# Feed-forward entries of a two-layer decoder: ScalarE empties the PSUM banks, and the first entry's normalisation takes its statistics from summed residuals and squares

## The chip, the cores and the metric

The kernel runs on one core of a Trainium2 chip. The metric is the device time of one execution in microseconds; the time of a kernel is the median of its runs. The core's engines are TensorE (PE, with its weight load PEld), VectorE (DVE), ScalarE (ACT), GpSimd (POOL) and SyncE (SP), which issues most of the transfers.

## The reference

Input and output are 1024 tokens of 1024 features in fp32. Two layers run one after the other; layer 0 mixes tokens by a gated linear recurrence, layer 1 by sliding-window attention. Each mixer ends in a projection `w_out`, and each layer ends in a gated feed-forward network of width 2816 with a causal depthwise convolution. Every sub-layer is joined to the stream in the same way:

```python
def layer_norm(x, g, b):
    mu = xf.mean(-1, keepdims=True)
    var = jnp.square(xf - mu).mean(-1, keepdims=True)
    y = (xf - mu) * lax.rsqrt(var + LN_EPS) * g + b
...
    # each sub-layer: x = layer_norm(ALPHA * x + sublayer(x), g, b)
```

What matters here is the join between a mixer's projection and the feed-forward network behind it: residual sum, normalisation over the 1024 features, and the first products of the network.

## The kernel before, in words

A block `tb` is 128 tokens, so there are 8 blocks; a row tile `Y[:, tb, :]` is 128 x 1024. fp32 matrix products are made as three matmuls (L222 to L224, `mm3`) of a high and a low part: ScalarE casts the high part (`nc.scalar.copy`, L249), VectorE subtracts it to get the low part (L197, `low_part`).

**The entry of a feed-forward network** is `out_proj` with the tasks `Up.ln(tb)` that it starts. `out_proj` makes the mixer's output projection in two halves of 512 columns, `dh` 0 and 1. Each product of a block is 24 matmuls into a 128 x 512 PSUM bank (`psmm`, four banks taken in turn; some of the first half's lie in `psax`). VectorE adds it to the residual (L380) and takes the statistics of that half row (`ln_half`, L263). In the second half the blocks come in the order 4, 5, 6, 7, 0, 1, 2, 3. After a block's second half, `Up.ln` runs `ln_affine`: the two half statistics are aggregated (L269), the variance gets its epsilon (L270), POOL takes the power −0.5 (L271), VectorE subtracts the mean and multiplies with gain (L280), then scales and adds bias (L283), and the rows are stored. Then the block waits until the order clock has gone on by 8 us (blocks 0 to 3) or 13 us (blocks 4 to 7; 10 in layer 1), and TensorE turns it: two halves of four 128 x 128 transposes each (`tr`, L232) into a bank apiece.

What is taken out of these banks: for blocks 0 to 3 the high part (ScalarE), the low part (VectorE, from the bank) and a copy of the turned rows (ScalarE, L433) into `hf`; for blocks 4 to 7 a copy of the first half (L435), and for the second half a high and a low part and the sum with the first half (L438, from the bank). L443 to L445 make further sums of turned blocks. They are the operands of the feed-forward products, in which seven block products stand for eight; the parts of the weights are summed by `weight_sums` (L480 to L483) and split like the rest. `collect` empties the later products' banks (L506 to L520), makes the convolution (L526, L528) and the gate (L531, L533).

**What sets the order.** Only TensorE's order is written by hand. Its work is spaced by a clock `od` that counts estimated work. On the other engines a scheduler orders the instructions by due times and priorities; what stands under `urgent()` is put forward. Each engine then executes in order and stops at the first instruction whose operands or target are not ready.

Names in the lists below: `Y_4374` holds the rows of blocks 4 to 7, `Y_4181` those of blocks 0 to 3, `rx_4698` to `rx_4700` are three tiles into which weights and rows are loaded, `HL` holds split weights (and one row of gains), `T` turned blocks, `st`, `mv` and `rs` are statistics, `gd` the network's hidden rows in HBM.

Of the kernel before, what the change touches and what calls it, by code (L numbers as in the profile page):

```python
# [10 lines left out]
F32 = mybir.dt.float32  # L11
# [5 lines left out]
P = 128  # L17
S = 1024
D = 1024
# [115 lines left out]
def trunk(ctx: ExitStack, tc: tile.TileContext, a: dict, out: bass.AP):  # L135
# [123 lines left out]
    def ln_half(tb, i):  # L259

        if tb not in half_stats:
            half_stats[tb] = sm.tile([P, 2, 6], F32, name="st", bufs=8)
        nc.vector.bn_stats(half_stats[tb][:, i, :], Y[:, tb, i * 512:(i + 1) * 512])  # L263
# [7 lines left out]
        nc.gpsimd.tensor_tensor(rs, rs, nhalf, op=ALU.pow)  # L271
        return mv, rs

    def ln_affine(tb, rows, dst, n=1):

        y = Y[:, tb, :]
        mv, rs = ln_stats(tb)
        parts = [slice(h * D // n, (h + 1) * D // n) for h in range(n)]
        for hs in parts:
            nc.vector.scalar_tensor_tensor(y[:, hs], y[:, hs], mv[:, 0:1], rows[0][:, hs],  # L280
                                           op0=ALU.subtract, op1=ALU.mult)
        for hs in parts:
            nc.vector.scalar_tensor_tensor(y[:, hs], y[:, hs], rs, rows[1][:, hs], op0=ALU.mult, op1=ALU.add)  # L283
            nc.sync.dma_start(dst(hs), y[:, hs])
# [71 lines left out]
    def out_proj(us, begun, rows, resid, ff, ln):  # L356
        tasks, late = [], []
        for tb in range(NB):
            nc.sync.dma_start(Y[:, tb, :], resid(tb))
        for tb, ps in enumerate(begun):  # L360
            out_part(ps, us, tb, [KC - 1])
        for dh in range(2):
            if dh:
                ff.row_loads()
                ff.weights(1)
            for tb in range(NB):
                if dh == 0 and tb < 4:
                    out_late(late, rows, tb, ff.TX)
                elif dh == 0 and tb == 4:
                    ff.weights(0)  # L370
                if dh:
                    tb = (tb + 4) % NB
                if dh == 0 and tb < len(begun):
                    ps = begun[tb]
                else:
                    ps = psmm()
                    out_part(ps, late if dh else us, tb, range(KC))
                y = Y[:, tb, dh * 512:(dh + 1) * 512]
                with urgent() if dh else nullcontext():
                    nc.vector.scalar_tensor_tensor(y, y, ALPHA, ps, op0=ALU.mult, op1=ALU.add)  # L380
                    ln_half(tb, dh)
                if dh == 1:
                    tasks.append(od.spawn(ln(tb)))
                    od.tick()
        return tasks
# [17 lines left out]
    class Up:  # L403
        def __init__(self, l, pool, rx):
            self.l, self.rx = l, rx
            self.wv = a["ffn_w_in"][l].rearrange("(kc p) c -> p kc c", p=P)
            self.TX = pool.tile([P, 2, 2, 4, 512], F32R, name="TX")
            self.T2 = pool.tile([P, 2, 4, 512], F32R, name="T2")
            self.W, self.raw, self.pieces = {}, {}, 0

        def row_loads(self):
# [5 lines left out]

        def ln(self, tb):
            with urgent():
                ln_affine(tb, self.rows, lambda hs: ynd[:, tb, hs], 2 if tb == 3 else 1)  # L420
            yield 8.0 if tb < 4 else 10.0 if self.l else 13.0
            turned = lambda t: (self.rx[2 * t - 4] if t in (2, 3) else Y[:, t, :]).rearrange("p (k t) -> p k t", k=KC)
            hf = turned(tb)
            ts = slice(tb * P, (tb + 1) * P)
            with urgent():
                for q in range(2):
                    ps, ks = psmm(), slice(4 * q, 4 * q + 4)
                    for k in range(4):
                        tr(ps[:, k * P:(k + 1) * P], Y[:, tb, (4 * q + k) * P:(4 * q + k + 1) * P])
                    pv = ps.rearrange("p (k t) -> p k t", k=4)  # L430
                    if tb < 4:
                        split(T[:, 0, ks, ts], T[:, 1, ks, ts], pv)
                        nc.scalar.copy(hf[:, ks], pv)  # L433
                    elif q == 0:
                        nc.scalar.copy(hf[:, ks], pv)  # L435
                    else:
                        split(T[:, 0, ks, ts], T[:, 1, ks, ts], pv)
                        tt(hf[:, ks], hf[:, :4], pv, op=add)  # L438
                        split(T[:, 0, :4, ts], T[:, 1, :4, ts], hf[:, ks])
                        return  # L440
            sf = turned(tb + 4)
            a11, a12, a21, s1 = hf[:, :4], hf[:, 4:], sf[:, :4], sf[:, 4:]
            tt(a21, a11, a21, op=sub)  # L443
            tt(a11, s1, a11, op=sub)
            tt(a12, a12, a11, op=sub)  # L445
            split(self.T2[:, 0, :, ts], self.T2[:, 1, :, ts], a21)
            yield 100.0
            pair = hf.rearrange("p (c k) t -> p c k t", c=2)
            split(self.TX[:, :, 0, :, ts], self.TX[:, :, 1, :, ts], pair)
# [1462 lines left out]
```

## Time and profile before

| | |
|---|---|
| median of 3 runs | 2120.18 us (2120.07 to 2121.75) |
| profiled execution | 2122.24 us, span 2120.4 us |
| mean granted TensorE clock | 0.996 |
| TensorE (PE) busy | 2091.9 us, 99% of the span |
| VectorE (DVE) busy | 1777.2 us, 84% |
| ScalarE (ACT) busy | 968.1 us, 46% |
| GpSimd (POOL) busy | 187.1 us, 9% |

A time in a row of the trace is counted from the span's start. A row of the timeline has start, duration, engine, line, operation, target and operands, shape and type, and in brackets the idle time before it with what ended it. "PEclk" is the granted clock as a share of full speed. Matmuls overlap their neighbours, so their spacing is read from start to start. The entry of layer 0's feed-forward network lies at about 476 to 556 us, that of layer 1's at about 1430 to 1530 us.

### The profile page before, as it was taken

What the parts mean: (1) busy time and instruction counts of PE and PEld (TensorE: products, weight loads), DVE (VectorE), ACT (ScalarE), POOL (GpSimd) and SP (SyncE); (2) the same over time, 40 slices, a digit from 0 to 9 for tenths busy, and PEclk for the clock granted to TensorE, in tenths of its full rate; (3) what the DMA queues carried; (4) which work ended last, traced back from release to release, by engine and by line L of the source; (5) the groups of instructions that cost most, each with busy time, mean ns of one, the idle gap of its engine ahead of it and who ended that gap; (6) DMA issues with size and microseconds to landing.
All of it is one profiled execution on the core that took longest, in us unless ns stands there. A gap on an engine that the chain in (4) does not pass through costs nothing. (4 is left out here: it accounts for less than half of the span.)

```text
span 2120.4 us, 31566 instructions
## 1 busy us (share of the span) xinstructions
PE 2091.9 (99%) x12303; PEld 1742.8 (82%) x12303; DVE 1777.2 (84%) x2420; ACT 968.1 (46%) x1562; POOL 187.1 (9%) x214
## 2 busy tenths in 40 slices
PE   9899999999999999999999999999999999999998
PEld 7688888887878888888888888888888888888886
DVE  6677777769989999888988668979999999978986
ACT  6455565543444444444433356743544444444430
POOL 1000000001010000000001122311010000000002
PEclk9999999999999999999999999999999999999999
DMA  4021111143247765628754511052266776449662
GB/s 153 21 71 50 51 51 51 66 169 110 90 124 174 194 156 150 157 98 294 268 189 159 159 34 38 23 156 93 85 167 167 177 174 161 123 152 326 225 207 98
DMA packets 239823, 286.82 MB, mean 135 GB/s; under 512 B 30216, under 2 KB 160440, under 8 KB 239416
## 3 DMA queue, kind: packets, MB, share of 16 engines
q1 hardware_dynamic: 223360, 238.26, 34.6%
q0 software_dynamic: 15456, 46.16, 10.9%
q8 instruction: 97, 1.59, 0.3%
q14 instruction: 54, 0.44, 0.1%
q10 hardware_dynamic: 856, 0.37, 0.1%
HBM read 241.72 MB, written 89.15 MB: 156 GB/s over the span
## 5 line engine op out<-in xcount | busy, mean ns | idle before, releaser
L222 PE MATMUL psmm<-T,HL 128*128 128x512 f32 x816 | 323.3, 396 | 5.2 <-ACT T L874 4.8
L223 PE MATMUL psmm<-T,HL 128*128 128x512 f32 x816 | 319.2, 391 | 1.3 <-DVE T L197 1.3
L224 PE MATMUL psmm<-T,HL 128*128 128x512 f32 x816 | 319.3, 391 | 0.2 <-DVE HL L197 0.2
L528 DVE SCALAR_TENSOR_TENSOR Y<-Y,cwt,Y 128x1023 f32<-128x1023 f32 (+1 forms) x176 | 225.1, 1281 | 49.7 <-ACT Y L526 48.3
L249 ACT CAST HL<-rx 128x1024 fp32r<-128x1024 f32 (+1 forms) x151 | 151.1, 1006 | 159.6 <-DMA rx<-in_ffn_w_in_dram 28.1
L197 DVE TENSOR_TENSOR HL<-rx,HL 128x1024 fp32r<-128x1024 f32 (+1 forms) x151 | 176.4, 1175 | 17.6 <-ACT HL L249 17.3
L222 PEld LDWEIGHTS psmm<-T,HL 128*128 128x128 f32 x816 | 153.9, 189 | 36.8 <-ACT T L874 5.2
L224 PEld LDWEIGHTS psmm<-T,HL 128*128 128x128 f32 x816 | 153.8, 188 | 33.0 <-DVE HL L197 0.6
L223 PEld LDWEIGHTS psmm<-T,HL 128*128 128x128 f32 x816 | 153.9, 189 | 32.8 <-DVE T L197 2.2
L222 PE MATMUL psax<-T,HL 128*128 128x512 f32 x392 | 153.5, 392 | 0.0
L223 PE MATMUL psax<-T,HL 128*128 128x512 f32 x392 | 152.9, 390 | 0.0
L224 PE MATMUL psax<-T,HL 128*128 128x512 f32 x392 | 152.7, 390 | 0.0
L526 ACT ACTIVATE Y<-Y,cwt 128x1024 f32<-128x1024 f32 x88 | 108.8, 1237 | 92.8 <-DVE Y L515 82.8
L197 DVE TENSOR_TENSOR HL<-raw,HL 128x512 fp32r<-128x512 f32 (+1 forms) x121 | 92.2, 789 | 40.6 <-ACT HL L1296 30.7
L271 POOL TENSOR_TENSOR rs<-rs,nhalf 128x1 f32<-128x1 f32 x32 | 45.0, 1407 | 735.3 <-DVE rs L270 735.3
L249 ACT CAST HT<-rx 128x1024 fp32r<-128x1024 f32 (+1 forms) x37 | 35.5, 960 | 139.2 <-DVE rx L482 61.9
L222 PEld LDWEIGHTS psax<-T,HL 128*128 128x128 f32 x392 | 73.8, 188 | 15.9 <-ACT Y L507 0.4
L222 PE MATMUL psmm<-HL 128*128 128x512 f32 x220 | 86.9, 395 | 0.0
L224 PEld LDWEIGHTS psax<-T,HL 128*128 128x128 f32 x392 | 73.8, 188 | 15.4
L223 PEld LDWEIGHTS psax<-T,HL 128*128 128x128 f32 x392 | 73.8, 188 | 15.2
L223 PE MATMUL psmm<-HL 128*128 128x512 f32 x220 | 85.9, 391 | 0.0
L224 PE MATMUL psmm<-HL 128*128 128x512 f32 x220 | 85.8, 390 | 0.0
(404 smaller groups left out, 5200.5 us busy)
## 6 DMA issues: line engine op xcount, KB each, us to landing
rx<-in_ffn_w_in_dram SPq DMA_DIRECT2D x136, 256.0 KB
rx<-gd SPq DMA_DIRECT2D x118, 256.0 KB
bsd<-in_ffn_w_out_dram POOLq DMA_DIRECT2D x36, 768.0 KB, 8.4
gd<-Y SPq DMA_DIRECT2D x44, 512.0 KB
raw<-in_hgrn_w_in_dram SPq DMA_DIRECT2D x30, 512.0 KB
rx<-in_ffn_w_out_dram SPq DMA_DIRECT2D x54, 256.0 KB
R<-bsd SPq DMA_DIRECT2D x44, 256.0 KB
Y<-in_ffn_w_in_dram SPq DMA_DIRECT2D x40, 256.0 KB
```

The lines of the kernel that those rows point to most:

```text
L197: make = lambda e: e.tensor_tensor(lo, src, hi.bitcast(F32), op=ALU.subtract)
L222: nc.tensor.matmul(ps, st(0), mv(0), start=start, stop=False, skip_group_check=onto)
L223: nc.tensor.matmul(ps, st(0), mv(1), start=False, stop=False, skip_group_check=onto)
L224: nc.tensor.matmul(ps, st(1), mv(0), start=False, stop=stop, skip_group_check=onto)
L249: nc.scalar.copy(hi, src)
L271: nc.gpsimd.tensor_tensor(rs, rs, nhalf, op=ALU.pow)
L526: nc.scalar.activation(c, u, AF.Identity, bias=cwt[:, l, 3, ci:ci + 1], scale=cwt[:, l, 2, ci:ci + 1])
L528: nc.vector.scalar_tensor_tensor(c[:, sh:], u[:, :S - sh], cwt[:, l, 2 - sh, ci:ci + 1], c[:, sh:], op0=ALU.mult, op1=ALU.add)
```

## The change: what it does

Three things are changed in the entries; TensorE's instructions and their order stay as they are.

1. *The second half's products.* ScalarE copies the bank into a new tile `lf` in SBUF (128 x 512, one buffer), and VectorE's residual sum reads `lf` (both layers).
2. *The turned rows.* ScalarE makes the high part and the plain copy of a bank; VectorE makes the low part from the copy in SBUF, and for blocks 4 to 7 the sum with the first half too (both layers).
3. *The statistics, layer 0 only.* The residual sums give out their row sums (`accum_out`); the 16 half-row statistics and 8 aggregations go. VectorE makes the negative mean (L294 of the changed kernel), ScalarE squares the two half rows with the mean as bias and gives out their sums (L296, the squares themselves go to a part of `T` that is not in use then), VectorE adds them (L298), POOL adds epsilon (L299) and takes the power (L300).

```diff
-    def ln_affine(tb, rows, dst, n=1):
+    def resid_half(tb, i, ps, summed):
+        y = Y[:, tb, i * 512:(i + 1) * 512]
+        if not summed:
+            nc.vector.scalar_tensor_tensor(y, y, ALPHA, ps, op0=ALU.mult, op1=ALU.add)
+            ln_half(tb, i)
+            return
+        if tb not in half_stats:
+            half_stats[tb] = sm.tile([P, 2, 6], F32, name="st", bufs=8)
+        nc.vector.scalar_tensor_tensor(y, y, ALPHA, ps, op0=ALU.mult, op1=ALU.add,
+                                       accum_out=half_stats[tb][:, 0, i:i + 1])
+
+    def square_stats(tb):
+        st = half_stats.pop(tb)
+        less = st[:, 0, 2:3]
+        rs = sm.tile([P, 1], F32, name="rs")
+        nc.vector.tensor_scalar(less, st[:, 0, 0:1], st[:, 0, 1:2], -1.0 / D, op0=ALU.add, op1=ALU.mult)
+        for i in range(2):
+            nc.scalar.activation(T[:, 1, :4, tb * P:(tb + 1) * P], fourths(Y[:, tb, i * 512:(i + 1) * 512]), AF.Square, bias=less,
+                                 accum_out=st[:, 1, i:i + 1])
+        nc.vector.tensor_scalar(rs, st[:, 1, 0:1], st[:, 1, 1:2], 1.0 / D, op0=ALU.add, op1=ALU.mult)
+        nc.gpsimd.tensor_scalar(rs, rs, 1.0, LN_EPS, op0=ALU.mult, op1=ALU.add)
+        nc.gpsimd.tensor_tensor(rs, rs, nhalf, op=ALU.pow)
+        return less, rs
+
+    def ln_affine(tb, rows, dst, n=1, summed=False):
         y = Y[:, tb, :]
-        mv, rs = ln_stats(tb)
+        if summed:
+            mean, rs = square_stats(tb)
+            from_it = ALU.add
+        else:
+            mv, rs = ln_stats(tb)
+            mean, from_it = mv[:, 0:1], ALU.subtract
...
-            nc.vector.scalar_tensor_tensor(y[:, hs], y[:, hs], mv[:, 0:1], rows[0][:, hs],
-                                           op0=ALU.subtract, op1=ALU.mult)
+            nc.vector.scalar_tensor_tensor(y[:, hs], y[:, hs], mean, rows[0][:, hs],
+                                           op0=from_it, op1=ALU.mult)
...
-                y = Y[:, tb, dh * 512:(dh + 1) * 512]
                 with urgent() if dh else nullcontext():
-                    nc.vector.scalar_tensor_tensor(y, y, ALPHA, ps, op0=ALU.mult, op1=ALU.add)
-                    ln_half(tb, dh)
+                    if dh:
+                        nc.scalar.copy(ff.left, ps)
+                        ps = ff.left
+                    resid_half(tb, dh, ps, ff.l == 0)
...
+            self.left = pool.tile([P, 512], F32, name="lf")
...
-                    if tb < 4:
-                        split(T[:, 0, ks, ts], T[:, 1, ks, ts], pv)
-                        nc.scalar.copy(hf[:, ks], pv)
-                    elif q == 0:
-                        nc.scalar.copy(hf[:, ks], pv)
-                    else:
-                        split(T[:, 0, ks, ts], T[:, 1, ks, ts], pv)
-                        tt(hf[:, ks], hf[:, :4], pv, op=add)
+                    if tb < 4 or q:
+                        nc.scalar.copy(T[:, 0, ks, ts], pv)
+                    nc.scalar.copy(hf[:, ks], pv)
+                    if tb < 4 or q:
+                        low_part(T[:, 1, ks, ts], hf[:, ks], T[:, 0, ks, ts], None)
+                    if tb >= 4 and q:
+                        tt(hf[:, ks], hf[:, :4], hf[:, ks], op=add)
                         split(T[:, 0, :4, ts], T[:, 1, :4, ts], hf[:, ks])
                         return
```

The scheduler's order on VectorE moves with it. At the place where block 0 is normalised in layer 0 (`Y_4181`), VectorE's rows stood so before:

```order
L380 SCALAR_TENSOR_TENSOR Y_4181<-Y_4181,psmm 128x512
L483 TENSOR_TENSOR rx_4700<-rx_4700,rx_4698 128x512
L197 TENSOR_TENSOR T<-Y_4374,T 128x4x128
L263 BN_STATS st<-Y_4181 128x6
L197 TENSOR_TENSOR T<-psmm,T 128x4x128
L269 BN_AGGR mv<-st 128x2
L438 TENSOR_TENSOR Y_4374<-Y_4374,psmm 128x512
L270 TENSOR_SCALAR rs<-mv 128x1
L280 SCALAR_TENSOR_TENSOR Y_4181<-Y_4181,mv,HL 128x1024
L197 TENSOR_TENSOR T<-Y_4374,T 128x4x128
L283 SCALAR_TENSOR_TENSOR Y_4181<-Y_4181,rs,rx_4699 128x1024
```

and stand so in the changed kernel (its L283 is the residual sum, L314 and L317 are the two steps that were L280 and L283, L473 was L438):

```order
L283 SCALAR_TENSOR_TENSOR Y_4181,st<-Y_4181,lf 128x512
L197 TENSOR_TENSOR T<-Y_4374,T 128x4x128
L294 TENSOR_SCALAR st<-st 128x1
L473 TENSOR_TENSOR Y_4374<-Y_4374 128x512
L197 TENSOR_TENSOR HL<-rx_4698,HL 128x1024
L197 TENSOR_TENSOR T<-Y_4374,T 128x4x128
L298 TENSOR_SCALAR rs<-st 128x1
L314 SCALAR_TENSOR_TENSOR Y_4181<-Y_4181,st,HL 128x1024
L283 SCALAR_TENSOR_TENSOR Y_4181,st<-Y_4181,lf 128x512
L317 SCALAR_TENSOR_TENSOR Y_4181<-Y_4181,rs,rx_4699 128x1024
```

Two rows (L294 and L298) now stand between the residual sum and L314, with ScalarE's squares between them; a low half of weights of 1024 columns (`HL<-rx_4698`) and block 1's residual sum stand ahead of block 0's last step, and another such half (`HL<-rx_4700`) stands some rows further ahead.

ScalarE's rows for the end of the entry, where block 2 is turned and block 3 is normalised, in the changed kernel (L414 is the copy into `lf`, L468 and L469 the high part and the copy of turned rows, L296 the squares):

```order
L414 COPY lf<-psmm 128x512
L468 CAST T<-psmm 128x4x128
L469 COPY rx_4698<-psmm 128x512
L468 CAST T<-psmm 128x4x128
L296 ACTIVATE T,st<-Y_4181,st 128x4x128
L469 COPY rx_4698<-psmm 128x512
L296 ACTIVATE T,st<-Y_4181,st 128x4x128
```

Block 3's squares stand behind casts and copies of block 2. Later, in the fourth of the network's product groups (at about 600 us before), VectorE's rows stood so before:

```order
L482 TENSOR_TENSOR Y_4374<-Y_4374,rx_4700 128x512
L197 TENSOR_TENSOR HL<-rx_4699,HL 128x512
L483 TENSOR_TENSOR rx_4700<-rx_4700,Y_4374 128x512
L528 SCALAR_TENSOR_TENSOR Y_4374<-Y_4181,cwt,Y_4374 128x1023
L518 TENSOR_TENSOR Y_4181<-Y_4181,psmm 128x1024
L528 SCALAR_TENSOR_TENSOR Y_4374<-Y_4181,cwt,Y_4374 128x1022
L520 TENSOR_TENSOR Y_4181<-Y_4181,psax 128x512
L197 TENSOR_TENSOR HL<-rx_4700,HL 128x1024
L197 TENSOR_TENSOR HL<-Y_4374,HL 128x1024
```

and stand so in the changed kernel (L517, L518, L553, L555 and L563 were L482, L483, L518, L520 and L528):

```order
L517 TENSOR_TENSOR Y_4374<-Y_4374,rx_4700 128x512
L563 SCALAR_TENSOR_TENSOR Y_4374<-Y_4181,cwt,Y_4374 128x1023
L548 TENSOR_TENSOR Y_4181<-Y_4181,psax 128x512
L563 SCALAR_TENSOR_TENSOR Y_4374<-Y_4181,cwt,Y_4374 128x1022
L518 TENSOR_TENSOR rx_4700<-rx_4700,Y_4374 128x512
L550 TENSOR_TENSOR Y_4181<-Y_4181,psmm 128x512
L197 TENSOR_TENSOR HL<-Y_4374,HL 128x1024
L197 TENSOR_TENSOR HL<-rx_4700,HL 128x1024
L563 SCALAR_TENSOR_TENSOR Y_4374<-Y_4181,cwt,Y_4374 128x1023
L553 TENSOR_TENSOR Y_4181<-Y_4181,psmm 128x1024
L563 SCALAR_TENSOR_TENSOR Y_4374<-Y_4181,cwt,Y_4374 128x1022
L555 TENSOR_TENSOR Y_4181<-Y_4181,psax 128x512
```

The low half `HL<-Y_4374` stands ahead of the half `HL<-rx_4700` and of four rows (two of the convolution, two sums of products) that it stood behind.

More of the change, by code (lines that the diff above doesn't have):

```diff
@@ L272, in ln_stats, with fourths @@
         return mv, rs
-    def ln_affine(tb, rows, dst, n=1):
-        y = Y[:, tb, :]
-        mv, rs = ln_stats(tb)
+    def resid_half(tb, i, ps, summed):
[8 more added lines that the diff above has]
+                                       accum_out=half_stats[tb][:, 0, i:i + 1])
+    def fourths(v):
+        return v.rearrange("p (k t) -> p k t", k=4)
+    def square_stats(tb):
[11 more added lines that the diff above has]
+    def ln_affine(tb, rows, dst, n=1, summed=False):
+        y = Y[:, tb, :]
+        if summed:
[4 more added lines that the diff above has]
+            mean, from_it = mv[:, 0:1], ALU.subtract
         parts = [slice(h * D // n, (h + 1) * D // n) for h in range(n)]
         for hs in parts:
-            nc.vector.scalar_tensor_tensor(y[:, hs], y[:, hs], mv[:, 0:1], rows[0][:, hs],
-                                           op0=ALU.subtract, op1=ALU.mult)
+            nc.vector.scalar_tensor_tensor(y[:, hs], y[:, hs], mean, rows[0][:, hs],
+                                           op0=from_it, op1=ALU.mult)
         for hs in parts:
@@ L419, in ln @@
             with urgent():
-                ln_affine(tb, self.rows, lambda hs: ynd[:, tb, hs], 2 if tb == 3 else 1)
+                ln_affine(tb, self.rows, lambda hs: ynd[:, tb, hs], 2 if tb == 3 else 1, self.l == 0)
             yield 8.0 if tb < 4 else 10.0 if self.l else 13.0
```

## The prediction

> **What bounds the kernel now.** I read the busy times and the waits of TensorE first, since an engine that is hardly ever idle can only be helped by taking its waits away.
>
> ```profile
> PE 2091.9 (99%) x12303; PEld 1742.8 (82%) x12303; DVE 1777.2 (84%) x2420; ACT 968.1 (46%) x1562; POOL 187.1 (9%) x214
> ```
>
> TensorE is busy 2091.9 of 2120.4 us. The change leaves its instructions and their order as they are, so it can only act through waits (some 28 us in all) and through the granted clock. The waits of TensorE by releaser (total, times, longest) say which of them the change touches:
>
> ```profile
> PE psmm L224 <- DVE HL L197: 2.9, 2, 2.7
> PE psmm L232 <- DVE Y L380: 1.6, 1, 1.6
> ...
> PE psmm L232 <- ACT Y L433: 1.2, 1, 1.2
> ...
> PE psmm L232 <- DVE Y L438: 0.4, 1, 0.4
> ```
>
> L232 are the turning instructions of the first feed-forward entry, which wait for a PSUM bank: L380 is VectorE's residual sum out of a bank, L438 its sum of turned rows, L433 a copy by ScalarE. The first row, 2.7 us in one piece, is a product's wait for the low half of a weight. The entry is the stretch from about 505 to 556 us; its first 36 us by engine (PE, PEld, DVE, ACT, POOL, then clock, DMA share and GB/s):
>
> ```profile
> 505.00:541.00 36.00, 32.52 (x166) 26.71 (x165) 35.70 (x56) 12.46 (x22) 7.32 (x5) 1.00 0.30 117
> ```
>
> VectorE is busy 35.70 of 36.00 there, ScalarE 12.46: a bank that VectorE is to empty stands in VectorE's queue. On TensorE itself:
>
> ```profile
> 516.00 0.60 PE L232 MATMUL psmm<-ident,Y 128*128 128x128 f32 x4
> 518.24 0.66 PE L232 MATMUL psmm<-ident,Y 128*128 128x128 f32 x4 [1.64 <-DVE Y L380]
> ...
> 530.50 1.04 PE L232 MATMUL psmm<-ident,Y 128*128 128x128 f32 x8
> 531.78 1.09 PE L232 MATMUL psmm<-ident,Y 128*128 128x128 f32 x8 [0.24 <-ACT Y L435]
> ```
>
> Eight turns last 1.04 us and four 0.60, so four more cost 0.44. Block 5's second half starts 2.24 us after its first: 1.80 late, 0.16 more than the wait shown. With the same 0.16 the waits of 0.4, 0.24 and 1.2 are 0.6, 0.4 and 1.35 late. **Bank waits of this entry: 4.1 us.**
>
> **What goes.** ScalarE now empties every bank of the entry (bar the early dh=0 products), and on the changed order its copy stands two or three rows behind what TensorE last wrote. So all 4.1 us of bank waits end. That gain is bounded by 0 and 4.1; I take 4.1, because ScalarE has 23 us free in the 36.
>
> The reads that move from PSUM to SBUF gain VectorE nothing:
>
> ```profile
> L263 DVE BATCH_NORM_STATS2 st<-Y 128x6 f32<-128x512 f32 x16 | 10.9, 686 | 0.0
> L197 DVE TENSOR_TENSOR T<-psmm,T 128x512 fp32r<-128x512 f32 x12 | 8.0, 675 | 0.5 <-ACT T L249 0.5
> L197 DVE TENSOR_TENSOR T<-Y,T 128x512 fp32r<-128x512 f32 x5 | 3.4, 687 | 0.0
> ```
>
> 675 ns from PSUM, 687 from SBUF. What VectorE loses is the 16 statistics rows of 686 ns, of which some nine fall behind 497.7 us.
>
> **What comes: the queue ahead of block 0.** Take away the bank waits and TensorE reaches block 0's turns at 531.78 − 0.24 − 1.80 − 0.60, about 529.0 us. They need block 0's normalised rows, and those come from VectorE's queue:
>
> ```profile
> 497.72 1.23 DVE L197 TENSOR_TENSOR HL<-rx,HL 128x1024 fp32r<-128x1024 f32 x1 [2.59 <-ACT HL L249]
> ...
> 501.26 0.20 DVE L269 BATCH_NORM_AGGREGATE mv<-st 128x2 f32<-128x12 f32 x1
> 501.38 0.69 DVE L482 TENSOR_TENSOR rx<-rx,rx 128x512 f32<-128x512 f32 x1
> 501.98 0.15 DVE L270 TENSOR_SCALAR rs<-mv 128x1 f32<-128x1 f32 x1
> 502.05 1.28 DVE L280 SCALAR_TENSOR_TENSOR Y<-Y,mv,HL 128x1024 f32<-128x1024 f32 x1
> 503.24 0.69 DVE L483 TENSOR_TENSOR rx<-rx,rx 128x512 f32<-128x512 f32 x1
> ...
> 529.84 1.28 DVE L283 SCALAR_TENSOR_TENSOR Y<-Y,rs,rx 128x1024 f32<-128x1024 f32 x1
> ```
>
> Start to start, a 512-column operation takes 0.60, a 1024-column one with a scalar 1.19, a tiny one 0.12. Before, block 0 was ready at 531.1; so even an unchanged queue would hold TensorE 2.1 us here. In the changed order the stretch from the row at 497.72 to block 0's last L317 holds 5 low halves of 1024 columns (1.13 each, by the two rows at 609.81 below), 10 operations of 1.19, 24 of 0.60 and 10 tiny ones: 5.65 + 11.9 + 14.4 + 1.2 = 33.2 us. No less than before (33.4, from 497.7 to 531.1), although the statistics are gone: two 1024-column weight halves, HL<-rx_4700 and HL<-rx_4698, now stand ahead of block 0 and stood behind it.
>
> To it come waits inside the queue. Each block's chain leaves VectorE and returns twice: L294 to ScalarE's two squares to L298, then POOL's L299 and L300 to L317. Their prices, by the nearest rows:
>
> ```profile
> L1016 ACT ACTIVATE kp<-fg,one 128x512 f32<-128x512 f32 x14 | 10.1, 722 | 0.5
> L1233 ACT ACTIVATION_READ_ACCUMULATOR sq<-psax 128x1 f32 x64 | 12.5, 196 | 0.0
> ...
> L271 POOL TENSOR_TENSOR rs<-rs,nhalf x32: 919/1452/1537, 502.2 to 2114.6; 128x1 f32<-128x1 f32 x32
> L1234 POOL TENSOR_SCALAR ss<-ss x8: 199/344/909, 114.1 to 468.0; 128x8 f32<-128x8 f32 x8
> ```
>
> Two squares with their read-outs are 2 × (0.72 + 0.20) = 1.84 us, POOL 0.34 + 1.45 = 1.79 where it was 1.45. Between L298 and L317 stand one 1.19 and one 0.60 operation, exactly 1.79, so a wait of 0.2 to 0.3 shows at each of four blocks; one block's L298 finds too little ahead of it, and a weight sum's low half waits for ScalarE's cast. I put 1.9 us for all (bounds 0 and 3). The residual sum with an accumulator has no row; its nearest, ScalarE's, is followed by a read-out row. If VectorE has one too, six lie ahead of block 0 at 0.12: 0.7 us (bounds 0 and 6 × 0.20 = 1.2). I take it. Block 0 is ready at 497.7 + 33.2 + 1.9 + 0.7 = 533.5: **a new wait of 4.5 us** (2.1 to 6.0) takes the place of the 4.1.
>
> **The clock.** One stretch shows a wait long enough to be punished, another one that isn't:
>
> ```profile
> 519.00:520.00 1.00, 1.00 (x6) 0.83 (x5) 1.00 (x3) 1.00 (x2) 0.00 (x0) 1.00 0.67 274
> ...
> 613.00:614.00 1.00, 1.00 (x4) 0.81 (x3) 1.00 (x3) 0.00 (x0) 0.00 (x0) 0.64 1.12 337
> 614.00:615.00 1.00, 1.00 (x4) 0.76 (x3) 1.00 (x1) 0.05 (x1) 0.00 (x0) 0.50 0.89 261
> ```
>
> ```profile
> 608.90 0.39 PE L222 MATMUL psmm<-TX,HL 128*128 128x512 f32 x1
> 609.13 0.39 PE L223 MATMUL psmm<-TX,HL 128*128 128x512 f32 x1
> 612.20 0.50 PE L224 MATMUL psmm<-TX,HL 128*128 128x512 f32 x1 [2.68 <-DVE HL L197]
> ...
> 616.88 0.40 PE L222 MATMUL psax<-T,HL 128*128 128x512 f32 x1
> ...
> 80.75 0.78 PE L222 MATMUL psmm<-T,HL 128*128 128x512 f32 x1 [4.79 <-ACT T L874]
> ...
> 87.63 0.40 PE L224 MATMUL psmm<-HL 128*128 128x512 f32 x1
> ```
>
> After the wait of 1.64 us the granted clock stays 1.00. After 2.68 us it falls to 0.50 at 614, and the 13 steps from 612.20 to 616.88 take 4.68 instead of 13 × 0.23 = 2.95: 1.7 lost. After 4.79 us the 14 steps to 87.63 take 6.88, of which 0.39 is another wait: 3.3 lost. For 4.5 us I take **1.8 us** (0 to 3.3), nearer the lower since turns and products just before keep the array busy. [...]
>
> **The last block.** Block 3's turns have no wait now, but little slack:
>
> ```profile
> 550.59 1.41 DVE L283 SCALAR_TENSOR_TENSOR Y<-Y,rs,rx 128x512 f32<-128x512 f32 x2
> ```
> ```profile
> 552.94 1.04 PE L232 MATMUL psmm<-ident,Y 128*128 128x128 f32 x8
> ```
>
> The rows end at 552.0, the turns start at 552.94: 0.9 us. The chain grows by ScalarE's copy into lf (0.5), the squares (1.84) queued behind a cast and a copy of block 2 (1.0), POOL's 0.34 and two tiny operations (0.2), and loses statistics of 0.6 + 0.2: 3.1 longer, so **2.2 us** late (0 to 3, nothing if ScalarE is free).
>
> **The wait at 609.** The product there stands still for HL<-Y, the second of these two rows:
>
> ```profile
> 601.94 2.62 DVE L482 TENSOR_TENSOR Y<-Y,rx 128x512 f32<-128x512 f32 x1
> ...
> 609.81 1.21 DVE L197 TENSOR_TENSOR HL<-rx,HL 128x1024 fp32r<-128x1024 f32 x1
> 610.94 1.21 DVE L197 TENSOR_TENSOR HL<-Y,HL 128x1024 fp32r<-128x1024 f32 x1
> ```
>
> In the changed order this low half stands ahead of HL<-rx, two convolution rows and two collecting sums that preceded it: 1.13 + 2 × 1.19 + 1.13 + 0.60 = 5.2 us earlier, about 606.9, where 609.4 is needed. The wait with its lateness (612.20 − 609.13 − 0.23 = 2.84) and its slow clock (1.73) go: **−4.6 us**. L482 (now L517) stands earlier too, behind fewer others, and must find its load landed; if not, the wait stays (bounds −4.6 and 0).
>
> **Layer 1's entry** gets the copy and the turned rows only; TensorE has no wait there now, and a chain longer by about 0.5 us stays inside it: 0.
>
> **Sum**: −4.1 + 4.5 + 1.8 + 2.2 − 4.6 = −0.2 us. Against the profiled execution's 2122.24 that is 2122.0. This execution lies 2.06 above the median, so on the median 2120.18 the forecast is **2120.0 us**: no change. About 0.2%, 4.2 us, is what a measurement of this kernel can tell from none.
>
> **Rivals.**
> *Block 0's queue at its floor.* If the accumulator costs nothing, the chain's waits are hidden and ScalarE serves block 3 in time, the terms are −4.1 + 2.1 + 0 + 0 − 4.6 = −6.6: 2113.6. For it: 23 us of idle ScalarE, and a wait of 2.1 lies between the 1.64 that kept the clock and the 2.68 that lost it. Against it: VectorE's in-order waits, four times. Chance 0.33.
> *The accumulating sum is slow (slower).* The residual sum now reads two fp32 arrays in SBUF and accumulates besides. If that takes it to half rate, each takes 0.53 us more (1.13 against 0.60); six before block 0 replace the read-outs' 0.7 by 3.2, the wait there is 7.0, its clock loss 3.3, and block 3 is 1.1 later with two more: −0.2 + 2.5 + 1.5 + 1.1 = +4.9, 2125.1. It decides from some 0.5 us an instruction. Against it: L280 reads two fp32 arrays in SBUF at the full 1.19 for 1024, but without an accumulator. Chance 0.14. [...]
> *The 609 wait stays*, since L517's load lands late: −0.2 + 4.6 = +4.4, 2124.6. Against it: L482 starts at 601.94 without a wait; how long its load had been there, no row shows. Chance 0.08.
> *The banks don't come free.* lf has one buffer, so ScalarE's copy may wait for VectorE's sum of the product before. Then the 4.1 stay as before, and block 0's wait shrinks by the same, since its queue sets its time: −0.2 again, 2120.0. It belongs to the forecast.
>
> **How the numbers follow.** Forecast 0.45, with its own range 2116 to 2124; the floor 0.33, slow accumulator 0.14, 609 wait 0.08. Faster takes the floor's share, all but a little, and the forecast's lower tail: 0.33. Slower takes most of the two last and the forecast's upper tail: 0.22. Same 0.45. The range runs from 2113.0 (a little under the floor rival) to 2125.3 (just above the slow one), which leaves out about a third of the floor's share and half of the slow one's.
>
> **What would show it.** Right: no L232 wait on VectorE's residual sum; a wait of 4 to 5 us at block 0's turns with 0.5 clock behind it; block 3's turns waiting some 2 us for L317; no 2.7 us wait in the fourth product group. Wrong: L283 rows of 1.1 us and more; block 0 ready before 531.5; a wait on lf; or new waits in layer 1's entry.

## The result

The changed kernel is slower: median 2125.72 us (11 runs, 2124.22 to 2128.32) against 2121.20 us for the kernel before on the same chips (11 runs). The ratio is 1.0023, 95% interval 1.0015 to 1.0031. The forecast was 2120.0 us and no change; the measured time lies 0.4 us above the range, and the likeliest case was the wrong one. The kernel before came out 1.0 us above the 2120.18 us on which the forecast stood, so the change itself costs 4.5 us by the medians. The profiled execution took 2125.27 us, its span is 2123.5 us.

The waits of TensorE in the changed kernel, by releaser (total, times, longest):

```profile
PE psmm L232 <- DVE st L294: 6.1, 1, 6.1
...
PE psmm L232 <- DVE Y L317: 1.3, 2, 0.9
...
PE psax L222 <- ACT Y L542: 1.2, 1, 1.2
...
PE psmm L232 <- ACT Y L469: 0.6, 1, 0.6
```

The residual sum, the sum of turned rows and the copies no longer hold TensorE, but for 0.6 us. The 2.7 us wait for a low half is gone. In their place stand one wait of 6.1 us, two for L317, and a new one in layer 1. On TensorE's timeline:

```profile
528.05 1.03 PE L232 MATMUL psmm<-ident,Y 128*128 128x128 f32 x8
535.14 1.94 PE L232 MATMUL psmm<-ident,Y 128*128 128x128 f32 x8 [6.05 <-DVE st L294]
543.47 1.03 PE L232 MATMUL psmm<-ident,Y 128*128 128x128 f32 x8
551.01 1.06 PE L232 MATMUL psmm<-ident,Y 128*128 128x128 f32 x8 [0.36 <-DVE Y L317]
558.48 1.14 PE L232 MATMUL psmm<-ident,Y 128*128 128x128 f32 x8 [0.93 <-DVE Y L317]
```

Block 0's eight turns last 1.94 instead of 1.03 us, and from them to the next block's it is 8.33 us, where 6.33 lie between other blocks (521.72 to 528.05): 2.0 us of slow clock. The first stretch of the entry and the fourth product group in windows (PE, PEld, DVE, ACT, POOL, clock, DMA share, GB/s):

```profile
505.00:541.00 36.00, 29.37 (x141) 24.42 (x141) 31.03 (x49) 22.16 (x47) 11.19 (x11) 0.91 0.25 93
...
600.00:620.00 20.00, 20.00 (x90) 16.57 (x89) 19.12 (x20) 9.00 (x10) 3.60 (x2) 1.00 0.32 106
```

VectorE fell from 35.70 to 31.03 us busy and is no earlier for it: it now stands still between its rows. What it stands still for is seen at block 0's last step:

```profile
531.00 0.21 DVE L298 TENSOR_SCALAR rs<-st 128x1 f32<-128x1 f32 x1
531.13 1.28 DVE L314 SCALAR_TENSOR_TENSOR Y<-Y,st,HL 128x1024 f32<-128x1024 f32 x1
532.32 0.69 DVE L283 SCALAR_TENSOR_TENSOR Y<-Y,lf 128x512 f32<-128x512 f32 x1
532.93 0.08 DVE L283 DVE_READ_ACCUMULATOR Y<-Y,lf 128x1 f32 x1
533.71 1.28 DVE L317 SCALAR_TENSOR_TENSOR Y<-Y,rs,rx 128x1024 f32<-128x1024 f32 x1 [0.70 <-POOL rs L300]
534.91 0.21 DVE L294 TENSOR_SCALAR st<-st 128x1 f32<-128x1 f32 x1
```
```profile
531.30 1.75 POOL L299 TENSOR_SCALAR rs<-rs 128x1 f32<-128x1 f32 x1 [5.87 <-DVE rs L298]
533.14 0.54 POOL L300 TENSOR_TENSOR rs<-rs,nhalf 128x1 f32<-128x1 f32 x1
```

From L298 to L317 it is 2.71 us; the rows between fill 1.8. POOL's two instructions did not run beside these rows. L299 starts 0.17 us behind the start of L314 and ends at 533.05, just behind the second of the rows (533.01), and only then comes the power, L300. In all eight blocks of the entry L299 ends 0.05 us behind the end of a VectorE row whose two tensor operands lie in SBUF: L314 alone, or the row after it too. The power takes 0.54 us when no such row runs; when one does, it takes 0.87 and ends 0.40 us behind the row. Two rows from elsewhere show that it is neither the idle stretch ahead of POOL nor just any row of VectorE. In the changed kernel at 467 us, after 45 us without work, a tiny instruction of POOL takes 0.20 us with VectorE at rest. In e8 (below), where block 1's residual sum reads a bank, the power keeps its 0.54 us beside that sum, and L317 follows 0.1 us behind it:

```profile
467.22 0.20 POOL L1269 TENSOR_SCALAR ss<-ss 128x8 f32<-128x8 f32 x1 [44.95 <-ACT sq L1268]
```
```profile
531.71 0.68 DVE L283 SCALAR_TENSOR_TENSOR Y<-Y,psmm 128x512 f32<-128x512 f32 x1
532.32 0.08 DVE L283 DVE_READ_ACCUMULATOR Y<-Y,psmm 128x1 f32 x1
532.50 1.28 DVE L317 SCALAR_TENSOR_TENSOR Y<-Y,rs,rx 128x1024 f32<-128x1024 f32 x1
```
```profile
531.92 0.54 POOL L300 TENSOR_TENSOR rs<-rs,nhalf 128x1 f32<-128x1 f32 x1
```

In the changed kernel L317 ends at 534.99, and the turns start at 535.14, though the profile puts the wait down to the next row on the queue, L294. Over the whole entry, VectorE's groups say the same:

```profile
L317 DVE SCALAR_TENSOR_TENSOR Y<-Y,rs,rx 128x1024 f32<-128x1024 f32 x7 | 9.0, 1285 | 4.1 <-POOL rs L300 3.4 <-DMA rx<-in_ln_mix_b_dram 0.7
...
L283 DVE SCALAR_TENSOR_TENSOR Y<-Y,lf 128x512 f32<-128x512 f32 x8 | 5.5, 687 | 0.4 <-ACT lf L414 0.4
...
L283 DVE DVE_READ_ACCUMULATOR Y<-Y,lf 128x1 f32 x8 | 0.7, 84 | 0.0
```

L317 waits 3.4 us for POOL, some 0.43 or 0.71 us at a time. The residual sum with an accumulator takes 687 ns from SBUF, as before from PSUM without one (678), and its read-out 84 ns that the next row covers.

In layer 1 ScalarE waits for a load ahead of the copies that empty a bank:

```profile
1569.34 0.62 ACT L249 CAST HT<-rx 128x512 fp32r<-128x512 f32 x1 [6.95 <-DMA rx<-in_ffn_w_in_dram]
...
1571.97 0.56 ACT L541 COPY Y<-psax 128x512 f32<-128x512 f32 x1
1572.43 0.58 ACT L542 COPY Y<-psax 128x512 f32<-128x512 f32 x1
```
```profile
1573.06 0.50 PE L222 MATMUL psax<-T,HL 128*128 128x512 f32 x1 [1.21 <-ACT Y L542]
```

Before, the same cast started at 1566.18, 3.2 us earlier, and TensorE had no wait there. TensorE itself is 1.9 us later here than before, and so is the first issue of the load (first the rows of SyncE's queue before, then of the changed kernel); the other 1.3 us lie between the issue and the cast, and why the load took longer the runs don't show:

```profile
1558.08 3.19 SPq L471 DMA_DIRECT2D rx<-in_ffn_w_in_dram  x4
```
```profile
1559.94 4.01 SPq L506 DMA_DIRECT2D rx<-in_ffn_w_in_dram  x4
```

### The profile page after: what moved, and what is told of

Its sections match the earlier page's. It is cut to its first block, busy times and chain, and to the rows that moved or that the text cites. A ratio compares the mean times of both kernels' runs of the same rounds, so it can differ in the third digit from the quotient of the medians.

```text
span 2123.5 us, 31638 instructions
## 1 busy us (share of the span) xinstructions
PE 2091.8 (99%) x12303; PEld 1742.0 (82%) x12303; DVE 1771.0 (83%) x2420; ACT 987.8 (47%) x1618; POOL 191.3 (9%) x222
## 5 line engine op out<-in xcount | busy, mean ns | idle before, releaser
L563 DVE SCALAR_TENSOR_TENSOR Y<-Y,cwt,Y 128x1023 f32<-128x1023 f32 (+1 forms) x176 | 225.3, 1282 | 49.7 <-ACT Y L561 48.2
L224 PEld LDWEIGHTS psmm<-T,HL 128*128 128x128 f32 x816 | 153.6, 188 | 33.2 <-DVE HL L197 0.6
L271 POOL TENSOR_TENSOR rs<-rs,nhalf 128x1 f32<-128x1 f32 x24 | 33.8, 1411 | 667.8 <-DVE rs L270 667.8
```

The lines of the kernel that those rows point to most:

```text
L224: nc.tensor.matmul(ps, st(1), mv(0), start=False, stop=stop, skip_group_check=onto)
L563: nc.vector.scalar_tensor_tensor(c[:, sh:], u[:, :S - sh], cwt[:, l, 2 - sh, ci:ci + 1], c[:, sh:], op0=ALU.mult, op1=ALU.add)
```

## The experiments

All eleven were timed beside the kernel before, in 11 runs each (e4 10, e7 7). Ratios are to it, with 95% intervals; a difference between two variants is taken between ratios, times 2121.

| kernel | median us | before us | ratio |
|---|---|---|---|
| changed kernel | 2125.72 | 2121.20 | 1.0023 (1.0015 to 1.0031) |
| e1 banks only, both layers | 2119.07 | 2120.89 | 0.9991 (0.9982 to 1.0000) |
| e2 statistics only | 2120.24 | 2120.89 | 0.9997 (0.9988 to 1.0006) |
| e3 change in layer 0 only | 2123.20 | 2120.89 | 1.0009 (1.0000 to 1.0018) |
| e4 epsilon on VectorE | 2125.99 | 2120.89 | 1.0024 (1.0015 to 1.0033) |
| e5 banks only, layer 0 only | 2116.38 | 2121.11 | 0.9977 (0.9968 to 0.9986) |
| e6 changed kernel without POOL's part | 2121.00 | 2121.11 | 0.9999 (0.9991 to 1.0008) |
| e7 lf and statistics | 2126.56 | 2121.11 | 1.0027 (1.0016 to 1.0037) |
| e8 turned rows and statistics | 2121.41 | 2121.11 | 1.0003 (0.9994 to 1.0012) |
| e9 lf in layer 1 alone | 2125.07 | 2120.73 | 1.0018 (1.0009 to 1.0027) |
| e10 turned rows in layer 0 alone | 2121.25 | 2120.73 | 1.0000 (0.9991 to 1.0009) |
| e11 e5 with sums on POOL | 2123.93 | 2120.73 | 1.0013 (1.0005 to 1.0022) |

**e1: the banks without the statistics.**

```diff
-                    resid_half(tb, dh, ps, ff.l == 0)
+                    resid_half(tb, dh, ps, False)
...
-                ln_affine(tb, self.rows, lambda hs: ynd[:, tb, hs], 2 if tb == 3 else 1, self.l == 0)
+                ln_affine(tb, self.rows, lambda hs: ynd[:, tb, hs], 2 if tb == 3 else 1)
```

> The statistics are as before (bn_stats, aggregation, POOL's power alone); only ScalarE's emptying of the banks is kept, in both layers. Theory (the squares, and POOL's two instructions in place of one, hold VectorE's queue ahead of block 0): the wait at block 0's turns falls from 6.05 us to about 2 (its queue sums to 32.7 us instead of 33.2 and loses 3.3 us of waits for POOL), no slow clock behind it, the 609 wait stays away (its low half stands early in this order too), layer 1 as in the changed kernel: -3.2 + 2.2 - 4.5 + 1.3, about 4 us below the kernel before. Rival (the copies into lf and out of the turned banks are what delays the blocks): a wait of 5 us or more stays at block 0 and the time is that of the changed kernel, 4 to 5 us above the kernel before.

1.8 us below the kernel before, at the edge of what can be told; about 4 was expected. The wait at block 0 is as expected, 2.0 us, one of three for L317. Of the two waits for L542, one of 0.4 is still in layer 0 (at 632 us); the other, 1.6, is layer 1's, where 1.3 was put in:

```profile
PE psmm L232 <- DVE Y L317: 3.6, 3, 2.0
PE psax L222 <- ACT Y L542: 2.0, 2, 1.6
```

VectorE runs its 32.9 us up to block 0 without a gap (496.22 to 529.07). The rival, that the copies delay the blocks, falls.

**e2: the statistics without the banks.** `ScalarE`'s copy into lf and the changed turned rows go back to what they were; `summed` stays.

```diff
-                    if dh:
-                        nc.scalar.copy(ff.left, ps)
-                        ps = ff.left
                     resid_half(tb, dh, ps, ff.l == 0)
...
```

> Only the summed residuals and the squares in layer 0; banks are emptied as before. Theory: VectorE's queue to block 0 sums to 31.5 us and keeps the waits for POOL (about 3 us), so block 0 is ready at about 533.5; the bank waits of 3 to 4 us come back ahead of it, so TensorE waits only some 2 us there; last blocks 1.6 late; the 609 wait stays away (-4.5); layer 1 as before (0). In sum -1 us, no change. Rival (the copies delay, the statistics help): 4 us or more below the kernel before.

0.65 us below the kernel before, no change, as expected:

```profile
PE psmm L232 <- DVE Y L317: 2.3, 2, 2.0
PE psmm L232 <- DVE Y L283: 2.2, 1, 2.2
```

The residual sum's bank holds TensorE for 2.2 us, and so it waits only 2.0 at block 0, which is ready at 532.07 (in this execution the clock falls even so: from 533.65 to 536.21 us the matmuls start 0.43 us apart, later 0.23). Each half of the change alone costs nothing; together they cost 4.5 us. With the banks free TensorE comes earlier, and block 0 is ready 2.9 us later than here.

**e3: layer 1 as before.**

```diff
-                    if dh:
+                    if dh and ff.l == 0:
                         nc.scalar.copy(ff.left, ps)
```

(and the turned rows as before where `self.l` is 1.)

> The changed kernel with layer 1 as before. Theory (ScalarE's and VectorE's shifted order in layer 1 makes a weight load land 1.3 us later at 1570 us): 1.3 to 1.6 us below the changed kernel, 3 us above the kernel before. Rival (the difference in layer 1 is carried over from layer 0 or is scatter): the time of the changed kernel, 4.5 us above the kernel before.

The ratio falls from 1.0023 to 1.0009, 3 us: rather more than the 1.3 to 1.6 expected. The wait of 6.0 at block 0 is unchanged, TensorE has no wait from 1425 to 1700 us. The intervals overlap (1.0015 and 1.0018), so this run alone would not settle it; e5 against e1, e9, and the profiles of e2 and e8 point the same way. From 1400 us to the end the changed kernel's profile loses 1.1 us against the kernel before, and this one gains 1.4: 2.4 us between the two.

**e4: epsilon on VectorE.**

```diff
-        nc.gpsimd.tensor_scalar(rs, rs, 1.0, LN_EPS, op0=ALU.mult, op1=ALU.add)
+        nc.vector.tensor_scalar(rs, rs, 1.0, LN_EPS, op0=ALU.mult, op1=ALU.add)
```

> The changed kernel with epsilon added by VectorE (a tiny instruction more in each block), so POOL makes the power alone. Theory (waits for POOL in VectorE's queue): the five waits for POOL ahead of block 0, 3.3 us in sum, fall to 1 or less, the tiny instructions cost 0.6, block 0 is ready about 2 us earlier, the wait there is about 4 us instead of 6.05, and the time 2 to 3 us below the changed kernel. Rival (the length of VectorE's queue alone counts, the waits are filled anyway): the queue is 0.6 us longer, the time 0.6 us above the changed kernel.

No gain, 1.0024: the expectation failed, and this run seemed to speak for the rival. Ahead of block 0 VectorE's rows keep the changed kernel's order, with the five epsilon rows in between. VectorE's waits for POOL there fell from 2.6 to 1.7 us, not to 1 or less: epsilon now stands behind L314, so the power starts beside the row that follows, it takes 0.85 to 0.93 us where in the changed kernel it took 0.54 with no such row, and L317 waits 0.42 to 0.45 us in each block. Block 0 was 0.7 us quicker on the queue (37.7 instead of 38.4 us), the wait there 5.7. Behind the entry the order moves, with a new wait of 0.7 us for L542 at 639 us, and in layer 1 that wait is 1.6 instead of 1.2. A run in which nothing but POOL goes was needed to tell the two apart.

**e6: no POOL at all.** Epsilon and the power are left out and the variance scales the rows, so this kernel does not normalise in layer 0; its time is a time without that part of the work. VectorE's and ScalarE's rows stand in the changed kernel's order.

```diff
         nc.vector.tensor_scalar(rs, st[:, 1, 0:1], st[:, 1, 1:2], 1.0 / D, op0=ALU.add, op1=ALU.mult)
-        nc.gpsimd.tensor_scalar(rs, rs, 1.0, LN_EPS, op0=ALU.mult, op1=ALU.add)
-        nc.gpsimd.tensor_tensor(rs, rs, nhalf, op=ALU.pow)
```

> The changed kernel without POOL's two instructions in layer 0: epsilon and the power are left out, the variance itself scales the rows. VectorE's and ScalarE's rows stand in the same order as in the changed kernel. Theory (VectorE stands still for POOL): the four waits of 2.6 us in sum ahead of block 0 go, with some small gaps, so block 0 is ready 2.5 to 3 us earlier, TensorE waits about 3 us there instead of 6.05, block 2 and 3 have no wait for L317 (-1.5), the clock falls less or not at all: 4 to 6 us below the changed kernel, about the time of the kernel before. Rival (VectorE's rows alone set the time, what it gains from POOL it waits for something else, as with epsilon on VectorE): within 1 us of the changed kernel.

5 us below the changed kernel (0.9999 against 1.0023), as expected. VectorE at block 0:

```profile
529.03 0.68 DVE L283 SCALAR_TENSOR_TENSOR Y<-Y,lf 128x512 f32<-128x512 f32 x1
529.64 0.08 DVE L283 DVE_READ_ACCUMULATOR Y<-Y,lf 128x1 f32 x1
529.64 1.28 DVE L315 SCALAR_TENSOR_TENSOR Y<-Y,rs,rx 128x1024 f32<-128x1024 f32 x1
```
```profile
531.07 1.49 PE L232 MATMUL psmm<-ident,Y 128*128 128x128 f32 x8 [3.75 <-DVE st L294]
```

The last step (L315 here) follows without a gap; the stretch from the first weight half to its end takes 35.3 us instead of 38.4. The wait is 3.75 instead of 6.05, and the turns of the later blocks wait for nothing. That VectorE stands still for POOL is shown, by a run in which the order of the other rows stays up to 1590 us. It is worth 3.1 us of queue and, with the clock and the last blocks, 5 us of time, in spite of a longer wait in layer 1 (2.1 us for the copy that was L542).

**e7 and e8: which of the copies.** e7 takes the turned rows out as before and keeps lf and the statistics; e8 leaves out lf and keeps the others.

```diff
# e7
-                    if tb < 4 or q:
-                        nc.scalar.copy(T[:, 0, ks, ts], pv)
-                    nc.scalar.copy(hf[:, ks], pv)
...
+                    if tb < 4:
+                        split(T[:, 0, ks, ts], T[:, 1, ks, ts], pv)
+                        nc.scalar.copy(hf[:, ks], pv)
...
# e8
-                    if dh:
-                        nc.scalar.copy(ff.left, ps)
-                        ps = ff.left
```

> The changed kernel with the turned rows taken out of their banks as before (VectorE reads the banks), so the copy into lf and the summed statistics are left. Theory (the order of VectorE's rows counts): its rows up to block 0 sum to 33.2 us as in the changed kernel, its waits for POOL stay, so block 0 is ready as late, about 535; some of TensorE's bank waits come back ahead of it, so the wait there is 4 to 5 us: 3 to 4.5 us above the kernel before. Rival (the extra copies of turned rows on ScalarE delay the squares): block 0 is ready about as early as with the statistics alone (532) and the time is that of the kernel before.

> The changed kernel without the copy into lf: VectorE's residual sum reads the bank again, the turned rows are taken out by ScalarE. Theory: VectorE's rows up to block 0 sum to 32.1 us, 1.1 less than in the changed kernel, and TensorE's wait of about 2 us for the residual sum's bank comes back ahead of block 0, so the wait there is 3 us or less and the clock stays or falls briefly: 0 to 2 us above the kernel before. Rival (the turned rows' copies delay): 4 us above the kernel before, as the changed kernel.

e7 is 5.7 us above the kernel before. At block 0 it is as expected (ready at 534.06, a wait of 4.5 us with a slow clock behind it, eight turns in 1.94 us). But the time has another share that was not expected, a low half in layer 1 that is 2.8 us late. e8 is at 1.0003 as expected, but not by the expected path: block 0 is ready at 533.8 and TensorE waits 4.6 us for it, not 3, and 1.5 us more at block 2; it makes up for that by having no wait at the residual sum's bank (2 us were put in), none at 609, and only 0.3 us in layer 1. The two differ in layer 1 by lf alone against the turned rows alone, and only lf loses there.

**e9: lf in layer 1 and nothing else.**

```diff
# against the kernel before
+                    if dh and ff.l == 1:
+                        nc.scalar.copy(ff.left, ps)
+                        ps = ff.left
```

> The kernel before with nothing but the copy into lf in layer 1's entry. Theory (this copy alone shifts VectorE's rows and the loads of weights in layer 1, so that a low half or a load is late at 1545 to 1570 us): layer 0 as before with its waits, in layer 1 a new wait of 1 to 3 us with or without a slow clock: 1.3 to 4.5 us above the kernel before. Rival (the loss in layer 1 needs the changed layer 0 ahead of it): the time of the kernel before.

1.0018, 3.8 us above the kernel before, inside the expected 1.3 to 4.5. Layer 0 has its old waits (the first of 0.8 instead of 1.6 us); layer 1 a new one, besides 0.5 at its turns. TensorE and VectorE there (POOL's gate L569 runs from 1537.64 for 2.41 us):

```profile
1548.25 0.50 PE L224 MATMUL psmm<-TX,HL 128*128 128x512 f32 x1 [2.82 <-DVE HL L197]
```
```profile
1537.99 2.61 DVE L518 TENSOR_TENSOR Y<-Y,rx 128x512 f32<-128x512 f32 x1
...
1545.85 1.21 DVE L197 TENSOR_TENSOR HL<-rx,HL 128x1024 fp32r<-128x1024 f32 x1
1546.98 1.21 DVE L197 TENSOR_TENSOR HL<-Y,HL 128x1024 fp32r<-128x1024 f32 x1
```

This is the wait at 609 of the kernel before, row for row, in the other layer: L518 beside POOL, and the low half HL<-Y behind two others. One copy more in an entry decides, 60 us later, on which side of the convolution rows this half is put. The rival, that layer 1 loses only with a changed layer 0 ahead of it, falls. But this is not the wait of the changed kernel, which is the one for L542 at 1573: that one stands, with 1.2 to 2.1 us, in the four kernels that have both copies in layer 1 (changed kernel, e1, e4, e6), and with 0.5 in e11, whose layer 1 is as before. So a loss of 3 to 4 us in layer 1 is shown, and by this run that the copy into lf alone is enough for it; by which wait it comes is not fixed.

**e5: the banks in layer 0 only**, which follows from e1 and e3.

```diff
# against the changed kernel
-                    if dh:
+                    if dh and ff.l == 0:
                         nc.scalar.copy(ff.left, ps)
                         ps = ff.left
-                    resid_half(tb, dh, ps, ff.l == 0)
+                    resid_half(tb, dh, ps, False)
```

(with the turned rows of layer 1 and the statistics as before.)

> Statistics as before in both layers, ScalarE empties the banks in layer 0 only. Theory (the banks alone gain, the squares cost, and layer 1's shift of its weight loads costs 1.3 to 1.6 us whatever layer 0 does): the time of the run with banks alone less 1.6, about 3.5 us below the kernel before; the wait at block 0 stays 2 us, without a slow clock. Rival (layer 1's loss is scatter of that profile): the same time as with the banks in both layers, 1.8 us below the kernel before.

0.9977, 4.9 us below the kernel before and some 10 us below the changed one: it beats both. The waits of TensorE that are left in the entry are for the blocks themselves:

```profile
PE psmm L232 <- DVE Y L317: 3.8, 3, 2.1
```

No bank wait, no wait at 609, none in layer 1, no slow clock in the entry (block 0's turns take 1.06 us). The last had some luck in it: the wait of 2.1 us at block 0 is about as long as the 2.0 of e2, behind which the clock fell (see the last section).

**e10 and e11: can e5 be had for less, or bettered?** e10 is e5 without lf; e11 is e5 with four weight sums on POOL.

```diff
# e10, against e5
-                    if dh and ff.l == 0:
-                        nc.scalar.copy(ff.left, ps)
-                        ps = ff.left
# e11, against e5
+            tt = nc.gpsimd.tensor_tensor if fc == 1 and self.l == 0 else nc.vector.tensor_tensor
```

> Only the turned rows of layer 0 are taken out by ScalarE; the residual sum reads its bank, statistics and layer 1 as before. Theory: VectorE's rows up to block 0 sum to 33.9 us (32.7 with the copy into lf), and the wait for the residual sum's bank (1.6 us) stays, so TensorE waits there and some 2 us at block 0; if the 609 wait goes, -4.5 + 1 = 3 us below the kernel before, and 1 us above the run with both copies in layer 0. Rival (the copy into lf is what brings the gain): the time of the kernel before.

> The run with the banks in layer 0 only, and the four weight sums of the second product group (512 columns each) on POOL, to shorten VectorE's queue ahead of block 0. Theory (the queue's rows set the remaining waits of 3.8 us): rows up to block 0 sum to 32.6 instead of 32.7, since others move up, so the wait at block 0 stays near 2 us, later ones shrink; POOL's operations beside VectorE's slow some of its rows: within 1.5 us of the run with the banks in layer 0. Rival (four rows less are four rows earlier): waits of 3.8 us fall by 2.4, 2 us below that run.

e10 gains nothing (1.0000), which is its rival's time: the bank waits go, the residual sum's too, which was to stay; but block 0's wait is 3.2 us, block 1's 0.7, and the wait at 609 is there again (2.8 us). The condition in its expectation did not hold. e11 loses 7.6 us against e5, and neither expectation covers that. POOL's four sums take 1.3 to 2.3 us each; a block's power starts only when the last of them is done (518.44 behind a sum of 2.13 from 516.34), TensorE waits at the turns of block 5 and again at block 0, where the clock falls to 0.50, and the wait at 609 is back:

```profile
PE psmm L232 <- DVE Y L317: 3.2, 1, 3.2
PE psmm L224 <- DVE HL L197: 2.6, 1, 2.6
PE psmm L232 <- ACT Y L481: 2.2, 2, 1.8
```

## Why the prediction was wrong, step by step

Lateness was followed from trace to trace by the start of the same matmul in both profiles, from 155 us on (where the changed kernel is 0.8 us ahead) to the end (2.7 behind): +3.6 us, where the forecast had −0.2.

- **Bank waits, −4.1: about −3.4.** All went but one, of 0.57 us.
- **"A new wait of 4.5 us" at block 0: 6.05. This is the step that failed.** The sum of VectorE's rows was right (33.2 us), and so was the place. The 0.7 us for the accumulators' read-outs came to nothing: a row with one takes 0.61 us from start to start, where one without takes 0.60. What failed is an overlap. The forecast let POOL's 1.79 us run beside 1.79 us of VectorE's rows and read off "a wait of 0.2 to 0.3". In the entry of the changed kernel the two did not run side by side where VectorE's row takes both operands from SBUF: L299 takes 0.6 to 1.8 us (1.31 in the mean, where 0.34 was put in) and ends 0.05 us behind such a row in all eight blocks, and L317 waits 0.43 us when the power is held by a row as well and 0.71 when it comes behind the last one. The rows that gave 0.34 have a spread of 0.20 to 0.91, and all but the shortest end 0.06 us behind a row of VectorE, so their median was no price. The change brought part of this itself: it moved the reads from banks to SBUF, which "gain VectorE nothing" but are among the rows behind which L299 ends (L473 at 524.07 us, L283 at 532.32). In e2, e7 and e8, where the row ahead of L317 reads a bank, L317 waits 0.10 to 0.12 us in six cases of six. So the term "I put 1.9 us for all (bounds 0 and 3)" was mis-sized: the stretch took 38.4 us, 5.2 on top of the rows, of which 2.6 are four gaps for POOL, 1.2 a load of the bias row and a cast, and 1.5 short gaps of under 0.2. The bound of 3 was too low for the same reason. The stretch was 2.6 us longer than forecast and began 1.1 us earlier (496.6, not 497.7), hence 1.5 us more of waiting. e6 shows POOL's part.
- **The clock, 1.8: 1.8 to 2.0,** by the lateness of the same matmuls and by the spacing of the turns. Right in size. It was an estimate between the two losses seen before, 1.7 and 3.3; that turns and products just ahead of a wait shorten the slow clock behind it, the reason given for the lower side, no run shows. A slow clock stood behind each of the entries' waits of 3.75 us and more (last section).
- **The last block, 2.2: about 1.6,** in two blocks (0.36 and 0.93, with the lateness around them). The mechanism was right: in e6 it goes with POOL. The two squares with their read-outs take 1.44 us from start to start, where 1.84 was put in.
- **The wait at 609, −4.6: −4.6.** Right; with the low half at 606.40 TensorE no longer stops. It was forecast from the changed order alone, and e10 and e11, where it stays, show how lightly it turns.
- **"Layer 1's entry: 0": +1.25 in the profile, 3 us in the time (e3).** The second failure. The entry itself has no wait, as said, but with the copies the rows and loads behind it stand otherwise, in the fourth and fifth product groups (e9 shows it for the copy into lf). The prediction looked for the price of the copies only in the entry.

These two put the forecast some 3 us too low, so that no change became a small loss. The rest of the lateness, some 0.6 us at about 670 us, wasn't forecast either. The two profiled executions lie 3.0 us apart and the medians 4.5; what makes up the difference no trace shows. Of the rivals, the floor (0.33) is near what the banks do without the statistics, in layer 0 only: −6.6 there, −4.9 in e5. The accumulator did cost nothing, as it had it; the waits weren't hidden. The slow accumulator is refuted by L283's 687 ns from two fp32 arrays in SBUF, 0.61 us from start to start, where the rival put 1.13. The loss came from waiting, not from a slow instruction.

By the ratios, the change is a sum of three: banks in layer 0 −4.9 us (e5), statistics on top of them +6.8 (e3 less e5), layer 1 +3.0 (changed kernel less e3). That the statistics cost nothing where the banks still hold TensorE (e2) follows from the waits: an earlier TensorE meets a later block 0. How much of block 0's lateness comes from the two rows that stand ahead of it in the changed order and not in e2's (1.7 us of row time) wasn't tried alone and stays open, as does why the scheduler's order places the late half of layer 1 so near the edge.

## What to carry to other kernels

Work taken off the busiest engine gains nothing if what replaces it makes that engine wait for two others in the middle of a chain: here VectorE's busy time in the entry's first 36 us fell from 35.70 to 31.03 us, and its stretch up to block 0 grew from 33.4 to 38.4. Before a round trip to another engine is laid beside rows, it has to be seen in a trace that the two run side by side: what an instruction ends with says more than its mean, and here a tiny POOL instruction ended 0.05 us behind VectorE's row, eight times of eight. And a small addition in one stage has to be looked for wherever a scheduler orders rows behind it, above all where a transfer or an operand was just in time.

## What was not expected of the hardware

**The clock didn't follow the length of a wait alone.** In e10 TensorE waited 3.18 us at block 0 and the clock stayed (1.00 from 532 to 536 us); in e11 it waited 3.17 at the same place and the clock was 0.50 behind it. Likewise 2.82 us at 1548 in e9 cost no clock (1.00 up to 1552), and 2.68 at 612 in the kernel before did (0.50 at 614). Shorter waits differ too: behind 2.03 us at block 0 in e2 the matmuls start 0.43 us apart, while the turns behind 2.12 at block 0 in e5 take 1.06 us for eight, and those behind 2.19 at 517 in e2 0.66 for four, as at full clock. Behind the waits of 3.75 us (e6), 4.48 (e7), 4.57 (e8), 5.66 (e4), 6.04 (e3) and 6.05 (changed kernel) at block 0, eight turns take 1.49 to 1.94 us instead of 1.03 to 1.06.

In the profiles of the kernel before and of the changed one, all changes of the granted clock lie whole multiples of 3.413 us apart: at 80.81, 87.63, 613.29, 616.70 and 2115.15 us before, at 78.40, 85.23, 532.38, 539.20 and 2119.57 in the changed kernel. In stretches of that length, counted from these changes, between 20 and 2100 us, the clock fell twice in each profile, at the end of stretches with 3.36 and 2.33 us of idle TensorE before and 2.18 and 3.29 in the changed kernel; it fell behind none of the other stretches at full clock, with 1.42 us or less. That the idle time within one stretch decides is a reading of these four falls. e10 and e11 agree with it: of e10's wait 1.76 us lie in the first of its windows here and 1.42 ahead of it, and e11's has 2.26 us in one (windows of 3.41 us, two of e10, then two of e11; the first figure behind the length is TensorE's busy time, the sixth, behind POOL's, the clock):

```profile
529.49:532.90 3.41, 1.65 (x12) 1.54 (x13) 3.08 (x5) 3.00 (x6) 0.30 (x1) 1.00 0.29 117
532.90:536.31 3.41, 3.41 (x17) 2.79 (x16) 3.41 (x7) 1.69 (x4) 0.79 (x1) 1.00 0.11 42
```
```profile
530.62:534.03 3.41, 1.15 (x10) 0.81 (x8) 3.41 (x7) 0.55 (x2) 1.45 (x1) 1.00 0.01 1
534.04:537.45 3.41, 2.52 (x10) 2.43 (x11) 3.31 (x7) 2.57 (x6) 0.16 (x1) 0.50 0.38 154
```

Where such stretches begin in e2 and e5 is not shown here.

**VectorE beside POOL.** VectorE was late behind POOL too. The profiles of the kernel before and of the changed one have eight gates by POOL. Beside seven of them, of 2.40 to 2.71 us, a row of VectorE with two operands in SBUF that starts while the gate runs takes 1.46 to 2.66 us for 512 columns and 2.84 to 3.43 for 1024, where 0.68 and 1.22 are usual, and ends 0.55 or 1.1 us behind the gate. Beside the eighth, at 593.27 before, the row keeps its 1.22 us and the gate takes 3.77. In the changed kernel the low half of 1024 columns takes 2.84 us, ending 1.1 us behind L568, and the next one 1.21.

```profile
606.40 2.84 DVE L197 TENSOR_TENSOR HL<-Y,HL 128x1024 fp32r<-128x1024 f32 x1
609.16 1.21 DVE L197 TENSOR_TENSOR HL<-rx,HL 128x1024 fp32r<-128x1024 f32 x1
```
```profile
605.45 2.71 POOL L568 TENSOR_TENSOR Y<-Y 128x1024 f32<-128x1024 f32 x1 [4.56 <-DVE Y L563]
```

The row at 601.94 before (2.62 us for 512 columns) and its twin in e9 both end 0.55 us behind such a gate.
